# Attention's scores with their 288 rows stacked as 128, 128 and 32, and two spans leaving PSUM in one instruction

## The chip, the core and the metric

The kernel runs on one core of a Trainium2 chip. The metric is device time in microseconds (us) of one execution, from a median of several runs. A core has five engines with their own instruction queues: TensorE (PE: matmuls, with weight loads shown as PEld), VectorE (DVE), ScalarE (ACT), GpSimd (POOL) and SyncE (SP, which here issues DMAs). Matmuls write to PSUM, which has 8 banks of 512 float32 a partition; VectorE and ScalarE read results from there into SBUF.

## The reference

One block of a bidirectional encoder: 1024 tokens of width 1024, with 16 learned tokens ahead of them (1040 keys), a retention branch and a latent attention branch that are merged by gates, then a feed-forward part. The part at hand is the attention of 8 heads. A head's query and key have 64 elements that come from a projection (`nope`) and 32 that are rotated by position (`rope`); the rotated key is shared by all heads.

```python
scale = MLA_QK ** -0.5
...
s = jnp.einsum('bqhd,bkhd->bhqk', qn, k_nope) + jnp.einsum('bqhr,bkr->bhqk', qr, k_rope)
p = jax.nn.softmax(s.astype(jnp.float32) * scale, axis=-1).astype(v.dtype)
return jnp.einsum('bhqk,bkhd->bqhd', p, v)
```

Everything is float32. The kernel multiplies numbers in a rounded float32 type (F32R in the code), and keeps accuracy by splitting an operand into a high part (the rounded number) and a low part (what is left). A product is then three matmuls: high by high, high by low, low by high.

## The kernel before

The program runs in stages: norm and combined projection, retention, latent projections, attention (from about 660 to 936 us), then the output projections and the feed-forward part. Only attention and what feeds it are touched.

*Operands.* For each head there are four SBUF tiles, `q[0]`, `q[1]` (96 x 1024, high and low) and `k[0]`, `k[1]` (96 x 1040). Rows 0 to 63 are the projected part, rows 64 to 95 the rotated part. `heads_begin` loads the rotated rows from DRAM (`qr_d` for queries, written by `rotary` as [half][high or low], and `kr_d` for keys, written by `shared_key`: eight loads a head), `heads_k` and `heads_q` compute the projected rows, in three column chunks each, from latents with a `gemm`; ScalarE rounds the high part, VectorE or GpSimd subtracts to get the low part. Heads come in pairs, and the pair after is prepared while the odd head of a pair is in work.

*Scores.* `softmax` handles one head and one block of 128 queries. The 1040 keys are three spans of 384, 384 and 272 (`ACH`), each in a PSUM bank of its own from the pool `ps_s` with three buffers. Each span is three matmuls of 96 rows (`mm3`, lines 140 to 142):

```python
mm3(ps[:, :n], q[0][:, t], q[1][:, t], k[0][:, c], k[1][:, c], True, True)
dve.tensor_scalar(pr[:, c], ps[:, :n], sq_c[:, qb : qb + 1], None, ALU.mult, ALU.max, accum_out=mx[:, j : j + 1])
```

The second line (line 1142) takes the span out of PSUM, multiplies by the query's norm factor `sq_c`, and leaves the span's maximum in `mx`. Line 1143 takes the maximum of the three with the sign turned (`nm`); line 1144 takes the exponential on ScalarE, in place, with the sum beside it.

*Turning and mixing.* `turn` transposes the eight 128 x 128 parts of a block on TensorE (line 1152, tiles `t`, pool `ps_t` with three buffers), ScalarE rounds them to `pth` (line 1154), VectorE subtracts to get `ptl` (line 1155). `turn_meta` does the same for the 16 extra keys, `inverse` gets the reciprocal of the sums to the right layout through DRAM (`l_d`, `lb`). `mix_values` multiplies the turned blocks by the values: 17 matmuls (lines 1181 and 1182) into a bank `o` of the pool `ps_o` (two buffers).

*Order.* The unit of the loop is one head and 256 queries (two blocks): 32 units. In the loop the scores of the next unit stand ahead of the turning of this one, and the mixing of the last unit comes after the first block's turning. The instructions are recorded by this code and then put in an order by a scheduler of the framework when the program is built; each engine runs its own queue strictly in that order, with semaphores for what one engine needs of another. So what stands next to what on TensorE is read from the built program's order, not from the code.

PSUM's eight banks in attention are three for `s`, three for `t`, two for `o`.

Of the kernel before, what the change touches and what calls it, by code (L numbers as in the profile page):

```python
# [18 lines left out]
NS, NT, NO = 3, 3, 2  # L19
D = 1024  # L20
S = 1024
NM = 16
L = S + NM
H = 8
KT = D // P
NB = S // P
# [4 lines left out]
BANK = {"11": "a", "t2": "b", "t3": "c", "n1": "d", "21": "a", "t4": "c", "22": "d"}  # L31
QCH = ((0, 384), (384, 384), (768, 256))
ACH = ((0, 384), (384, 384), (768, 272))


LINE = 16
# [14 lines left out]
def build(nc, tc, A, out):  # L51
# [26 lines left out]
    load = nc.sync.dma_start  # L78
    store = nc.sync.dma_start

    def f(t):
        return t.bitcast(F32)
# [175 lines left out]
    with ExitStack() as c1:  # L258
# [740 lines left out]
        wt = sb(rot, "rotary", 1, side="right")  # L999
        rr_ = sb(rot, "rotary_r", 11, side="right")  # L1000

        qr_d = [[mk(dram, (P, S), f"qr{i}{j}") for j in range(2)] for i in range(2)]
        wx, xx, tables = [], {}, []

        def wx_load(i):
# [8 lines left out]
        def rotary(lo, n, i):  # L1014
            c = slice(lo, lo + n)
            if i == 0:
                tables[:] = slot(rr_), slot(rr_)
                load(tables[0], A["cM"][:, c])
                load(tables[1], A["sM"][:, c])
            ta, tb_ = slot(rr_), slot(rr_)  # L1020
            dve.tensor_mul(ta, xx[lo, i], tables[0])
            dve.tensor_mul(tb_, xx[lo, 1 - i], tables[1])
            (dve.tensor_add if i else dve.tensor_sub)(ta, ta, tb_)
            hi = tb_.bitcast(F32R)
            act.copy(hi, ta)
            dve.tensor_sub(ta, ta, tb_)
            store(qr_d[i][0][:, c], tb_)
            store(qr_d[i][1][:, c], ta)

        ret_out(0)  # L1030
        seven_out(seven(w7, A["w_ro"][1], Z), cr, ret_post(1))
# [40 lines left out]

    with ExitStack() as c1:
        qk = sb(c1, "qk", 3)
        vp = sb(c1, "v", 1)
        vt = mk(vp, (P, NB + 1, H, P), "vt", F32R)
        pool.memset(f(vt)[:, NB], 0.0)
# [4 lines left out]
        ps_s = sb(c1, "ps_s", NS, space=PSUM)  # L1082
        ps_o = sb(c1, "ps_o", NO, space=PSUM)
        ps_t = sb(c1, "ps_t", NT, space=PSUM)

# [4 lines left out]
        def heads_begin(p):  # L1090
            wq = weights(wa, A["w_uq"][p], 384, "q")
            wk = weights(wa, A["w_uk"][p], 256, "k")
            for h in range(2):
                hh = 2 * p + h
                q = [mk(qk, (96, S), f"q{j}", F32R) for j in range(2)]
                k = [mk(qk, (96, 1152), f"k{j}", F32R)[:, :L] for j in range(2)]
                for j in range(2):
                    load(f(k[j])[64:80], kr_d[j][0:16])
                    load(f(k[j])[80:96], kr_d[j][32:48])
                    for i in range(2):  # L1100
                        load(f(q[j])[64 + 16 * i : 80 + 16 * i], qr_d[i][j][hh * 16 : hh * 16 + 16])
                qk_t[hh] = (q, k)
            return wq, wk

        def heads_k(p, wk, lo, n):
            c = slice(lo, lo + n)
            ps = mk(*((ps_o, (P, 512), "o") if p else (ps_t, (P, 512), "t")))
            gemm(ps[:, :n], wk, ckv, 2, lo, n)
            for h in range(2):
                k = qk_t[2 * p + h][1]  # L1110
                hs = slice(64 * h, 64 * h + 64)
                kf = mk(w2, (64, 384), "kf")
                dve.tensor_mul(kf[:, :n], ps[hs, :n], skv_b[hs, c])
                act.copy(k[0][0:64, c], kf[:, :n])
                pool.tensor_sub(k[1][0:64, c], kf[:, :n], f(k[0])[0:64, c])

        def heads_q(p, wq, lo, n):
            c = slice(lo, lo + n)
            ps = mk(*((ps_o, (P, 512), "o") if p else (ps_t, (P, 512), "t")))
            gemm(ps[:, :n], wq, cq, 3, lo, n)  # L1120
            for h in range(2):
                q = qk_t[2 * p + h][0]
                hs = slice(64 * h, 64 * h + 64)
                act.copy(q[0][0:64, c], ps[hs, :n])
                if p == 0 or h == 0:
                    dve.tensor_sub(q[1][0:64, c], ps[hs, :n], f(q[0])[0:64, c])
# [3 lines left out]
                pool.tensor_sub(q[1][0:64, c], qf[:, :n], f(q[0])[0:64, c])  # L1130

        def softmax(hh, qb, s, sums):
            q, k = qk_t[hh]
            t = slice(qb * P, (qb + 1) * P)
            mx = mk(w4, (P, 3), "mx")
            nm = mk(w4, (P, 1), "nm")
            pr = mk(w4, (P, L), "pr")
            for j, (lo, n) in enumerate(ACH):
                ps = mk(ps_s, (P, 512), "s")
                c = slice(lo, lo + n)  # L1140
                mm3(ps[:, :n], q[0][:, t], q[1][:, t], k[0][:, c], k[1][:, c], True, True)
                dve.tensor_scalar(pr[:, c], ps[:, :n], sq_c[:, qb : qb + 1], None, ALU.mult, ALU.max, accum_out=mx[:, j : j + 1])  # L1142
            dve.tensor_reduce(nm, mx, axis=AX.X, op=ALU.max, negate=True)  # L1143
            act.activation(pr, pr, AF.Exp, bias=nm, accum_out=sums[:, s : s + 1])  # L1144
            return pr

        def turn(pr, s, pt):
# [17 lines left out]
        def inverse(hh, qc, sums):  # L1165
            sm = mk(w4, (P, 2), "sm")
            dve.reciprocal(sm, sums)
            tp = mk(ps_t, (P, 4, P), "t")
            pe.transpose(tp[:2, 0, :], sm, ident)
            rr = mk(w4, (2, P), "rr")  # L1170
            act.copy(rr, tp[:2, 0, :])
            store(l_d[hh, 2 * qc : 2 * qc + 2], rr)
            lb = mk(w4, (64, 256), "lb")
            load(lb, l_d[hh, 2 * qc : 2 * qc + 2].rearrange("b i -> (b i)").unsqueeze(0).broadcast_to([64, 256]))
            return lb

        def mix_values(hh, qc, pt, lb):
            po = mk(ps_o, (P, 512), "o")
            for b in range(NB):
                for j in range(2):  # L1180
                    pe.matmul(po[:, :256], vt[:, b, hh, :], pt[j][:, b, :], start=(b == 0 and j == 0), stop=False)  # L1181
            pe.matmul(po[:, :256], vt[:, NB, hh, :], pt[2], start=False, stop=True)
            ta, tb_ = mk(w2, (64, 256), "oa"), mk(w2, (64, 256), "ob")
            act.copy(ta, po[64:128, :256])
            act.copy(tb_, po[0:64, :256])  # L1185
            pool.tensor_add(ta, ta, tb_)  # L1186
            hs = slice((hh % 2) * 64, (hh % 2) * 64 + 64)
            c = slice(qc * 256, qc * 256 + 256)
            if hh < H - 2:
                pool.tensor_mul(ta, ta, lb)  # L1190
                store(o_d[hh // 2, hs, c], ta)
            else:
                pool.tensor_mul(o3[qc // 2][hs, (qc % 2) * 256 : (qc % 2) * 256 + 256], ta, lb)
# [7 lines left out]
        sums_t, lb_t = {}, {}  # L1201

        def soft(unit, s):
            hh, qc = unit
            if s == 0:
                sums_t[unit] = mk(w4, (P, 2), "sums")
            return softmax(hh, 2 * qc + s, s, sums_t[unit])

        cur = [soft(units[0], s) for s in range(2)]

# [16 lines left out]

        wnext, late, o_s = None, None, []

        def mix(what):  # L1230
            if what:
                hh, qc, pt = what
                mix_values(hh, qc, pt, lb_t[hh, qc])

        for i, (hh, qc) in enumerate(units):
            nxt = units[i + 1] if i + 1 < len(units) else None
# [37 lines left out]
        mix(late)  # L1274


    with ExitStack() as c1:
# [348 lines left out]
```

## Time and profile before

| | us |
|---|---|
| time, median of 3 runs | 1725.82 |
| lowest and highest run | 1722.62, 1725.92 |
| the profiled execution's own time | 1727.16 |
| its span, first to last instruction | 1725.4 |
| stretch 0 to 660 (norm, projections, retention): TensorE busy | 637.5 |
| stretch 690 to 936 (attention): length | 246.0 |
| stretch 936 to the end (output, feed-forward): TensorE busy | 778.1 |

The granted clock of TensorE is at 0.99 to 1.00 throughout. In the rows of the profile a group is `line engine op out<-in`, with the names of the program's tiles; for a matmul `96*128 96x384` means 96 rows by 128 columns of the stationary operand, and 384 columns streamed from 96 rows. A matmul's shown duration includes the way through the array, so that rows that follow each other overlap: what a matmul costs in a stream is the distance to the next one's start. An entry `A <- B` of the waits means that A stood still until B was done.

### The profile page before, as it was taken

The page shows a single profiled execution, that of the slowest core. Times are in us where ns is not written, and L with a number is a line of the kernel's source. Part 1 is how long each engine was busy: PE and PEld are TensorE (multiplying, and loading weights), DVE is VectorE, ACT ScalarE, POOL GpSimd, SP SyncE. Part 2 cuts the span into 40 slices and gives each one's busy share as a digit, 9 for nine tenths or more (in the row PEclk, how much of TensorE's full clock was granted, in tenths as well). Part 3 has the DMA queues.
Part 4 walks back from the last instruction along what each step waited for, and adds up shares of the span by engine and source line. Part 5 has one row for each costly group of instructions (what it writes and reads, how often), then busy time and mean ns, then how long its engine had stood idle before and what let it go on. Part 6 is the DMA issues. An engine that isn't in the chain of part 4 may idle for free.

```text
span 1725.4 us, 26240 instructions
## 1 busy us (share of the span) xinstructions
PE 1686.0 (98%) x8657; PEld 1422.0 (82%) x8657; DVE 1355.5 (79%) x2484; ACT 838.5 (49%) x1581; POOL 740.4 (43%) x562
## 2 busy tenths in 40 slices
PE   9999999999998999999999999999999999999998
PEld 7888777888886777999998888888888888788787
DVE  8856698889899766988897769866788777866865
ACT  7535576433435424788886346333333333522335
POOL 0340377665644421323322401566666665423421
PEclk9999999999999999999999999999999999999999
DMA  8876734565647775111123744333444444876612
GB/s 287 286 272 196 246 129 147 172 219 199 221 140 274 233 243 174 32 49 29 29 84 116 241 151 147 101 101 98 135 146 141 140 147 162 305 269 210 227 59 98
DMA packets 169913, 287.15 MB, mean 166 GB/s; under 512 B 20841, under 2 KB 46882, under 8 KB 169778
## 3 DMA queue, kind: packets, MB, share of 16 engines
q1 hardware_dynamic: 168338, 284.15, 49.4%
q8 instruction: 68, 1.11, 0.3%
q10 hardware_dynamic: 1440, 1.33, 0.2%
q14 instruction: 67, 0.55, 0.1%
HBM read 193.28 MB, written 92.06 MB: 165 GB/s over the span
## 4 chain that ended last, share of the span: by engine, by line
PE 55%; DVE 4%; DMA 3%; ACT 1%; issue 1%; POOL 0%; SPq 0%; DVEq 0%; ACTq 0%
PE mm L223 32%; PE mm L140 3%; PE mm L141 3%; PE mm L142 3%; PE o L1181 3%; PE t L1152 3%; PE s L140 2%; PE s L141 1%; PE s L142 1%; DMA slot<-fl_d 1%; DVE slot L156 1%; DMA slot<-f_d 1%; DVE pr L1142 1%; PE o L140 1%; PE o L141 1%
## 5 line engine op out<-in xcount | busy, mean ns | idle before, releaser
L223 PE MATMUL mm<-slot,slot 128*128 128x512 f32 x2604 | 595.0, 390 | 3.6 <-DVE slot L216 1.8
L223 PEld LDWEIGHTS mm<-slot,slot 128*128 128x128 f32 x2604 | 487.2, 188 | 110.3 <-DVE slot L216 4.4
L216 ACT CAST slot<-slot 128x512 fp32r<-128x512 f32 (+1 forms) x385 | 226.2, 596 | 444.6 <-PE mm L223 345.6
L216 DVE TENSOR_TENSOR slot<-slot,slot 128x512 fp32r<-128x512 f32 (+1 forms) x385 | 351.9, 918 | 69.4 <-ACT slot L216 68.6
L196 POOL TENSOR_TENSOR slot<-slot,slot 128x512 f32<-128x512 f32 (+1 forms) x54 | 78.8, 1459 | 334.9 <-DMA slot<-in_w_g 79.2
L223 PE MATMUL mm<-ht,slot 128*128 128x512 f32 x552 | 184.8, 397 | 4.8 <-ACT slot L216 3.2
L223 PE MATMUL mm<-h,slot 128*128 128x512 f32 x440 | 152.9, 406 | 9.9 <-DVE slot L216 6.8
L214 POOL TENSOR_TENSOR slot<-slot,slot 128x512 f32<-128x512 f32 (+1 forms) x54 | 72.0, 1334 | 144.5 <-DVE slot L216 99.3
L156 DVE TENSOR_TENSOR slot<-slot,slot 128x512 fp32r<-128x512 f32 x123 | 98.9, 822 | 38.1 <-ACT slot L156 35.4
L223 PEld LDWEIGHTS mm<-ht,slot 128*128 128x128 f32 x552 | 103.1, 188 | 28.2 <-ACT slot L216 4.1
L156 ACT CAST slot<-slot 128x512 fp32r<-128x512 f32 x123 | 74.7, 620 | 77.6 <-POOL slot L1326 23.1
L223 PEld LDWEIGHTS mm<-h,slot 128*128 128x128 f32 x440 | 83.8, 192 | 30.9 <-DVE slot L216 9.6
L223 PE MATMUL mm<-lt,slot 128*128 128x512 f32 x276 | 108.5, 393 | 0.0
L141 PE MATMUL mm<-slot,slot 128*128 128x512 f32 (+1 forms) x288 | 105.3, 366 | 0.0
L142 PE MATMUL mm<-slot,slot 128*128 128x512 f32 (+1 forms) x288 | 105.3, 365 | 0.0
L140 PE MATMUL mm<-slot,slot 128*128 128x512 f32 (+1 forms) x288 | 105.2, 367 | 0.0
L1142 DVE TENSOR_SCALAR_CACHE_REDUCE pr<-s,sq_c 128x384 f32<-128x384 f32 (+1 forms) x192 | 101.9, 573 | 3.3 <-PE s L142 1.5
L197 POOL TENSOR_TENSOR slot<-slot,slot 128x512 f32<-128x512 f32 (+1 forms) x54 | 78.2, 1448 | 46.0 <-DVE slot L216 44.1
L1155 DVE TENSOR_TENSOR ptl<-t,pth 128x512 fp32r<-128x512 f32 x128 | 84.6, 685 | 11.3 <-ACT pth L1154 10.3
L223 PE MATMUL mm<-l,slot 128*128 128x512 f32 x220 | 88.1, 401 | 0.0
L1186 POOL TENSOR_TENSOR oa<-oa,ob 64x256 f32<-64x256 f32 x32 | 23.7, 742 | 144.9 <-ACT ob L1185 144.9
L1144 ACT ACTIVATE pr<-pr,nm 128x1040 f32<-128x1040 f32 x64 | 74.5, 1165 | 16.9 <-DVE nm L1143 16.8
(418 smaller groups left out, 3627.2 us busy)
## 6 DMA issues: line engine op xcount, KB each, us to landing
slot<-in_w_in SPq DMA_DIRECT2D x89, 256.0 KB
f_d<-slot SPq DMA_DIRECT2D x71, 256.0 KB
slot<-f_d SPq DMA_DIRECT2D x71, 256.0 KB
slot<-in_xT SPq DMA_DIRECT2D x48, 256.0 KB
slot<-in_w_g SPq DMA_DIRECT2D x44, 256.0 KB
slot<-in_w_u SPq DMA_DIRECT2D x44, 256.0 KB
fl_d<-slot SPq DMA_DIRECT2D x42, 256.0 KB
slot<-fl_d SPq DMA_DIRECT2D x42, 256.0 KB
```

Source lines behind the costliest of these rows:

```text
L140: pe.matmul(ps, sh, mh, start=start, stop=False)
L141: pe.matmul(ps, sh, ml, start=False, stop=False)
L142: pe.matmul(ps, sl, mh, start=False, stop=stop)
L156: split.done = act.copy(hi, t), dve.tensor_sub(lo, t, f(hi))
L196: adds.tensor_add(s1, a21, a22)
L197: adds.tensor_sub(s2, s1, a11)
L214: adds.tensor_sub(s2, s2, a12)
L216: split.done = act.copy(hi, side[b]), dve.tensor_sub(low, side[b], f(hi))
L223: split.mm = pe.matmul(ps, sw[:, ks], sx, start=begins and q == qs[0] and i == 0, stop=q == nq - 1 and i == 2, skip_group_check=True)
L1142: dve.tensor_scalar(pr[:, c], ps[:, :n], sq_c[:, qb : qb + 1], None, ALU.mult, ALU.max, accum_out=mx[:, j : j + 1])
L1144: act.activation(pr, pr, AF.Exp, bias=nm, accum_out=sums[:, s : s + 1])
L1155: dve.tensor_sub(pt[1][d], tp, f(pt[0])[d])
```

## The change

*Rows.* A score is a sum over 288 products of rows: 64 projected and 32 rotated, three times each. Before, they are three matmuls of 96 rows. Now they are two matmuls of 128 rows and one of 32. `q[0]` holds the projected high part over the projected low part, against `k[0]`, which holds the projected high part twice. `q[1]` holds projected high, rotated high and rotated low, against projected low, rotated low and rotated high in `k[1]`. What is left is rotated high by rotated high, 32 rows. The doubled rows are copied from SBUF to SBUF by SyncE's DMAs (one in `heads_k` and one in `heads_q` for each head and column chunk).

*The 32 rows.* The rotated high keys are loaded once into `kr` (96 x 384): the 32 rows of span 0 at partitions 0 to 31, of span 1 at 32 to 63, of span 2 at 64 to 95. The rotated high queries of a unit are loaded three times, to the same three places, into `rq` (three loads a unit, pool `ro` with three buffers). So the 32-row matmuls of the three spans lie on different rows of the array. `qr_d` gets another shape, so that a head's 32 rows are one load.

*Spans and PSUM.* The spans are 352, 352 and 336. The first two lie in one two-bank tile `s` (pool `ps_s`, one buffer), the third in a bank `u` (pool `ps_u`, one buffer). One VectorE instruction takes 704 columns out of `s`, one takes 336 out of `u`. The norm factor now carries a minus sign, so the instruction keeps a minimum, and the exponential turns the sign back.

*Mixing.* The 17 matmuls of `mix_values` are recorded in two portions, 8 after the first block's turning and 9 after the second's. `mx`, `rr` and `lb` get two buffers in place of four.

```diff
-    latent_norm(sq_c, 3, 96.0**-0.5, range(NB))
+    latent_norm(sq_c, 3, -(96.0**-0.5), range(NB))
...
+        kr = mk(vp, (96, 384), "kr", F32R)
+        for j, n in enumerate(SPANS):
+            for i in range(2):
+                load(f(kr)[32 * j + 16 * i : 32 * j + 16 * i + 16, :n],
+                     kr_d[0][32 * i : 32 * i + 16, SN * j : SN * j + n])
+        ps_s = sb(c1, "ps_s", 1, space=PSUM)
+        ps_u = sb(c1, "ps_u", 1, space=PSUM)
...
+                load(f(k[0])[64:128, c], f(k[0])[0:64, c])
...
+                load(f(q[1])[0:64, c], f(q[0])[0:64, c])
...
+        def rotary_queries(hh, qc):
+            t = mk(ro, (96, 256), "rq", F32R)
+            for j in range(3):
+                load(f(t)[32 * j : 32 * j + 32],
+                     qr_d[0][hh, :, :, qc * 256 : qc * 256 + 256].rearrange("i r t -> (i r) t"))
+            return t
...
-            for j, (lo, n) in enumerate(ACH):
-                ps = mk(ps_s, (P, 512), "s")
-                c = slice(lo, lo + n)
-                mm3(ps[:, :n], q[0][:, t], q[1][:, t], k[0][:, c], k[1][:, c], True, True)
-                dve.tensor_scalar(pr[:, c], ps[:, :n], sq_c[:, qb : qb + 1], None, ALU.mult, ALU.max, accum_out=mx[:, j : j + 1])
+            pa, pb = mk(ps_s, (P, 2, 512), "s"), mk(ps_u, (P, 512), "u")
+            spans = [(ps, slice(SN * j, SN * j + n)) for j, (ps, n) in
+                     enumerate(zip((pa[:, 0, :SN], pa[:, 1, :SN], pb[:, : SPANS[2]]), SPANS))]
+            for ps, c in spans:
+                for i in range(2):
+                    pe.matmul(ps, q[i][:, t], k[i][:, c], start=i == 0, stop=False)
+            for j, (ps, c) in enumerate(spans):
+                r = slice(32 * j, 32 * j + 32)
+                softmax.mm = pe.matmul(ps, rq[r, s * P : s * P + P], kr[r, : SPANS[j]], start=False, stop=True)
+            col = sq_c[:, qb : qb + 1]
+            dve.tensor_scalar(pr[:, : 2 * SN].rearrange("p (j n) -> p j n", n=SN), pa[:, :, :SN], col, None,
+                              ALU.mult, ALU.min, accum_out=mx[:, 0:1])
+            dve.tensor_scalar(pr[:, 2 * SN :], pb[:, : SPANS[2]], col, None, ALU.mult, ALU.min, accum_out=mx[:, 1:2])
...
-                if s == 0:
-                    mix(late)
+                mix(late, s, nxt)
```

The work ahead of attention and behind it keeps its order. Inside attention, TensorE's queue at one block of scores in the middle of the first head (tiles with their numbers; `s` are scores, `o` the mixing, `t` the transposes), before:

```order
L140 MATMUL s_7279<-k_1408_6774,q_1406_6772 128x384
L141 MATMUL s_7279<-k_1409_6775,q_1406_6772 128x384
L142 MATMUL s_7279<-k_1408_6774,q_1407_6773 128x384
L140 MATMUL s_7284<-k_1408_6774,q_1406_6772 128x384
L141 MATMUL s_7284<-k_1409_6775,q_1406_6772 128x384
L142 MATMUL s_7284<-k_1408_6774,q_1407_6773 128x384
L140 MATMUL s_7289<-k_1408_6774,q_1406_6772 128x272
L141 MATMUL s_7289<-k_1409_6775,q_1406_6772 128x272
L142 MATMUL s_7289<-k_1408_6774,q_1407_6773 128x272
L1182 MATMUL o_7251<-ptm_1399_6742,vt_6739 128x256
L1152 MATMUL t_7296<-ident_60,pr_7168 128x128 x4
L1152 MATMUL t_7303<-ident_60,pr_7168 128x128 x4
```

And the same block now (`kr` and `rq` are the operands of 32 rows):

```order
L1165 MATMUL s_7284<-k_1407_6785,q_1405_6783 128x352
L1165 MATMUL s_7284<-k_1408_6786,q_1406_6784 128x352
L1165 MATMUL s_7284<-k_1407_6785,q_1405_6783 128x352
L1165 MATMUL s_7284<-k_1408_6786,q_1406_6784 128x352
L1168 MATMUL s_7284<-kr_6746,rq_7236 128x352 x2
L1165 MATMUL u_7285<-k_1407_6785,q_1405_6783 128x336
L1165 MATMUL u_7285<-k_1408_6786,q_1406_6784 128x336
L1168 MATMUL u_7285<-kr_6746,rq_7236 128x336
L1182 MATMUL t_7299<-ident_60,pr_7173 128x128 x4
L1219 MATMUL o_7272<-ptm_1397_6743,vt_6740 128x256
L1182 MATMUL t_7306<-ident_60,pr_7173 128x128 x4
L1199 MATMUL t_7331<-ident_60,sm_7329 2x128
```

The code records the three 32-row matmuls behind all six others, but the scheduler has put the third span's two 128-row matmuls between the second and the third of them: the 32-row matmuls stand in 127 separate places for 64 blocks (two places a block, one in the first block). VectorE's queue at the same block, before:

```order
L1142 TENSOR_SCALAR pr_7278,mx_7276<-s_7279,sq_c_77 128x384
L1142 TENSOR_SCALAR pr_7278,mx_7276<-s_7284,sq_c_77 128x384
L1142 TENSOR_SCALAR pr_7278,mx_7276<-s_7289,sq_c_77 128x272
L1143 TENSOR_REDUCE nm_7277<-mx_7276 128x1
L1155 TENSOR_TENSOR ptl_7215<-t_7296,pth_7214 128x4x128
L1155 TENSOR_TENSOR ptl_7215<-t_7303,pth_7214 128x4x128
```

And now:

```order
L1170 TENSOR_SCALAR pr_7283,mx_7281<-s_7284,sq_c_77 128x704
L1172 TENSOR_SCALAR pr_7283,mx_7281<-u_7285,sq_c_77 128x336
L1173 TENSOR_REDUCE nm_7282<-mx_7281 128x1
L1185 TENSOR_TENSOR ptl_7234<-t_7299,pth_7233 128x4x128
L1185 TENSOR_TENSOR ptl_7234<-t_7306,pth_7233 128x4x128
L1197 RECIPROCAL sm_7439<-sums_7235 128x2
```

The three evictions have become two, at the same place in the queue; what follows them is unchanged.

More of the change, by code (lines that the diff above doesn't have):

```diff
@@ L18 @@
 P = 128
-NS, NT, NO = 3, 3, 2
+NT, NO = 3, 2
 D = 1024
@@ L33 @@
 ACH = ((0, 384), (384, 384), (768, 272))
+SN, SPANS = 352, (352, 352, 336)
 LINE = 16
@@ L1000, in build @@
         rr_ = sb(rot, "rotary_r", 11, side="right")
-        qr_d = [[mk(dram, (P, S), f"qr{i}{j}") for j in range(2)] for i in range(2)]
+        qr_d = [mk(dram, (H, 2, 16, S), f"qr{j}") for j in range(2)]
         wx, xx, tables = [], {}, []
@@ L1026, in rotary @@
             dve.tensor_sub(ta, ta, tb_)
-            store(qr_d[i][0][:, c], tb_)
-            store(qr_d[i][1][:, c], ta)
+            store(qr_d[0][:, i, :, c], tb_)
+            store(qr_d[1][:, i, :, c], ta)
         ret_out(0)
@@ L1074, in build @@
         qk = sb(c1, "qk", 3)
+        ro = sb(c1, "rotary_q", 3)
         vp = sb(c1, "v", 1)
@@ L1081, in build @@
             pool.memset(f(t), 0.0)
-        ps_s = sb(c1, "ps_s", NS, space=PSUM)
+        kr = mk(vp, (96, 384), "kr", F32R)
[5 more added lines that the diff above has]
+        ps_u = sb(c1, "ps_u", 1, space=PSUM)
         ps_o = sb(c1, "ps_o", NO, space=PSUM)
@@ L1094, in heads_begin @@
                 hh = 2 * p + h
-                q = [mk(qk, (96, S), f"q{j}", F32R) for j in range(2)]
-                k = [mk(qk, (96, 1152), f"k{j}", F32R)[:, :L] for j in range(2)]
+                q = [mk(qk, (P, S), f"q{j}", F32R) for j in range(2)]
+                k = [mk(qk, (P, 1152), f"k{j}", F32R)[:, :L] for j in range(2)]
                 for j in range(2):
-                    load(f(k[j])[64:80], kr_d[j][0:16])
-                    load(f(k[j])[80:96], kr_d[j][32:48])
                     for i in range(2):
-                        load(f(q[j])[64 + 16 * i : 80 + 16 * i], qr_d[i][j][hh * 16 : hh * 16 + 16])
+                        r = slice(64 + 32 * j + 16 * i, 80 + 32 * j + 16 * i)
+                        load(f(k[1])[r], kr_d[1 - j][32 * i : 32 * i + 16])
+                    load(f(q[1])[64 + 32 * j : 96 + 32 * j], qr_d[j][hh].rearrange("i r t -> (i r) t"))
                 qk_t[hh] = (q, k)
@@ L1133, in softmax @@
+        def softmax(hh, qb, s, sums, rq):
             q, k = qk_t[hh]
             t = slice(qb * P, (qb + 1) * P)
-            mx = mk(w4, (P, 3), "mx")
+            mx = mk(w2, (P, 2), "mx")
             nm = mk(w4, (P, 1), "nm")
             pr = mk(w4, (P, L), "pr")
-            for j, (lo, n) in enumerate(ACH):
-                ps = mk(ps_s, (P, 512), "s")
-                c = slice(lo, lo + n)
-                mm3(ps[:, :n], q[0][:, t], q[1][:, t], k[0][:, c], k[1][:, c], True, True)
-                dve.tensor_scalar(pr[:, c], ps[:, :n], sq_c[:, qb : qb + 1], None, ALU.mult, ALU.max, accum_out=mx[:, j : j + 1])
@@ L1145, in softmax @@
+            dve.tensor_reduce(nm, mx, axis=AX.X, op=ALU.min)
+            act.activation(pr, pr, AF.Exp, bias=nm, scale=-1.0, accum_out=sums[:, s : s + 1])
             return pr
@@ L1169, in inverse, with mix_begin, mix_some, mix_values @@
             pe.transpose(tp[:2, 0, :], sm, ident)
-            rr = mk(w4, (2, P), "rr")
+            rr = mk(w2, (2, P), "rr")
             act.copy(rr, tp[:2, 0, :])
             store(l_d[hh, 2 * qc : 2 * qc + 2], rr)
-            lb = mk(w4, (64, 256), "lb")
+            lb = mk(w2, (64, 256), "lb")
             load(lb, l_d[hh, 2 * qc : 2 * qc + 2].rearrange("b i -> (b i)").unsqueeze(0).broadcast_to([64, 256]))
             return lb
-        def mix_values(hh, qc, pt, lb):
+        def mix_begin(hh, qc, pt):
             po = mk(ps_o, (P, 512), "o")
-            for b in range(NB):
+            mix_some(po, hh, pt, range(4))
+            return po
+        def mix_some(po, hh, pt, bs):
+            for b in bs:
                 for j in range(2):
                     pe.matmul(po[:, :256], vt[:, b, hh, :], pt[j][:, b, :], start=(b == 0 and j == 0), stop=False)
+        def mix_values(po, hh, qc, pt, lb):
+            mix_some(po, hh, pt, range(4, NB))
             pe.matmul(po[:, :256], vt[:, NB, hh, :], pt[2], start=False, stop=True)
@@ L1200, in build @@
         units = [(hh, qc) for hh in range(H) for qc in range(4)]
-        sums_t, lb_t = {}, {}
+        sums_t, lb_t, rq_t = {}, {}, {}
         def soft(unit, s):
@@ L1206, in soft @@
                 sums_t[unit] = mk(w4, (P, 2), "sums")
-            return softmax(hh, 2 * qc + s, s, sums_t[unit])
+                rq_t[unit] = rotary_queries(hh, qc)
+            return softmax(hh, 2 * qc + s, s, sums_t[unit], rq_t[unit])
         cur = [soft(units[0], s) for s in range(2)]
@@ L1228, in build, with mix @@
         wnext, late, o_s = None, None, []
-        def mix(what):
-            if what:
+        open_ = []
+        def mix(what, s, nxt):
+            if not what:
+                return
+            if s == 0:
+                open_.append(mix_begin(*what))
+            else:
                 hh, qc, pt = what
-                mix_values(hh, qc, pt, lb_t[hh, qc])
+                mix_values(open_.pop(), hh, qc, pt, lb_t[hh, qc])
         for i, (hh, qc) in enumerate(units):
@@ L1273, in build @@
             cur = new
-        mix(late)
+        for s in range(2):
+            mix(late, s, None)
     with ExitStack() as c1:
```

7 lines of the change are left out of this document (2 added, 5 removed).

## The prediction

> **What bounds the kernel now.** I read the page's head first, then the table by stretches of time, then who waits for whom inside the attention stage, then the instructions of TensorE in order of time. The profiled execution took 1727.16 us, with a span of 1725.4, so 1.8 us lie around the span; the sum below starts from 1727.16, which stands 1.3 us above the median of 1725.82. Page and stretches (microseconds, then busy time and count of each engine):
>
> ```profile
> PE 1686.0 (98%) x8657; PEld 1422.0 (82%) x8657; DVE 1355.5 (79%) x2484; ACT 838.5 (49%) x1581; POOL 740.4 (43%) x562
> ...
> 660.00:690.00 30.00, 27.75 (x149) 23.91 (x148) 20.91 (x50) 16.49 (x30) 7.12 (x9) 1.00 0.40 117
> 690.00:936.00 246.00, 242.67 (x1824) 234.78 (x1824) 220.22 (x661) 199.47 (x437) 70.25 (x89) 1.00 0.15 44
> ```
>
> The change touches only attention, which is the stretch from 690 to 936 with its start from 660. There TensorE is busy 242.7 of 246.0 us at full clock, and VectorE 220.2. What TensorE waits for in that stretch is short (total, times, longest):
>
> ```profile
> PEld s L140 <- DVE pr L1142: 2.4, 8, 0.5
> PEld o L1181 <- ACT pth L1154: 2.1, 4, 0.7
> PEld t L1160 <- ACT rr L1171: 1.6, 4, 0.5
> ```
>
> So in attention time is what TensorE's queue adds up to. One block of scores, TensorE's rows in order (start, duration):
>
> ```profile
> 746.47 0.34 PE L140 MATMUL s<-k,q 96*128 96x384 f32 x1
> 746.65 0.34 PE L141 MATMUL s<-k,q 96*128 96x384 f32 x1
> ...
> 747.52 0.28 PE L140 MATMUL s<-k,q 96*128 96x272 f32 x1
> 747.64 0.29 PE L141 MATMUL s<-k,q 96*128 96x272 f32 x1
> 747.77 0.29 PE L142 MATMUL s<-k,q 96*128 96x272 f32 x1
> 747.89 0.29 PE L1182 MATMUL o<-ptm,vt 128*128 128x256 f32 x1
> 748.02 1.04 PE L1152 MATMUL t<-ident,pr 128*128 128x128 f32 x8
> 748.89 0.27 PE L1169 MATMUL t<-ident,sm 128*2 128x128 f32 x1
> ```
>
> Durations overlap, so cost is start to start. The nine matmuls of a block take 747.89 - 746.47 = 1.42 us: six of 384 columns at (747.52 - 746.47)/6 = 0.175, three of 272 at 0.123. There are 64 blocks.
>
> **The change, part by part.** *Streaming.* A column costs (0.175 - 0.123)/112 = 0.46 ns, so 352 columns cost 0.160 us and 336 cost 0.152. The six full-height matmuls take 4 x 0.160 + 2 x 0.152 = 0.944. Behind them come three of 32 rows. In the new order two stand next to each other and the third alone, behind the full-height ones of its own span. Matmuls on different rows of the array are in the trace: the retention stage has pairs of 64 rows (L744), one on rows 0 to 63 and one on 64 to 127 (two records for each matmul). Rows at 413 us, and the durations (min/median/max) of all of L744:
>
> ```profile
> 413.96 0.39 PE L223 MATMUL mm<-lt,slot 128*128 128x512 f32 x1
> 414.19 0.40 PE L223 MATMUL mm<-ht,slot 128*128 128x512 f32 x1
> 414.52 1.33 PE L744 MATMUL mm<-rq,rk 64*128 64x128 f32 x16
> 415.78 0.50 PE L223 MATMUL mm<-ht,slot 128*128 128x512 f32 x1
> 416.12 0.40 PE L223 MATMUL mm<-lt,slot 128*128 128x512 f32 x1
> ...
> L744 PE MATMUL mm<-rq,rk x128: 272/272/373, 295.4 to 471.0; 64*128 64x128 f32 x128
> ```
>
> The 16 start (1.33 - 0.37)/15 = 0.064 us apart; full-height ones of the same 128 columns, the eight transposes at 748.02, (1.04 - 0.27)/7 = 0.11 apart. So neighbours on different rows run side by side. Two 32-row matmuls then cost little over one, 0.17, and the third 0.152. Streaming alone goes from 1.42 to 0.944 + 0.32 = 1.264, a gain of 0.156 a block, **-10.0 us** in all.
>
> *Changing the height.* The same rows show what it costs to go to partial rows and back. At one height the start after 414.19 would be 0.23 later, at 414.42; the first 64-row matmul starts at 414.52, and takes 0.373 instead of 0.272. By ends: 414.59 for the last full one, 414.52 + 0.37 = 414.89 for the first partial one, of which its 128 columns stream 0.06; the array streams nothing for 0.24 us. On the way back the sixteen end at 415.85 and the next full one at 416.28, 0.43 later where 0.23 is usual: 0.20. No wait explains it, since the weight load ahead of the sixteen is put down to its own issue:
>
> ```profile
> 414.51 1.14 PEld L744 LDWEIGHTS mm<-rq,rk 64*128 64x128 f32 x16 [0.36 <-issue]
> ```
>
> Its start at 414.51 also shows that it was not pulled ahead of the running matmul, as the others are. A visit to another height thus costs 0.24 + 0.20 = 0.44 us beyond its streaming. In the new order a block makes two visits, one for the pair and one for the third; once in the program all three stand together, so 127 visits: **+55.9 us**. Nothing hides it, since TensorE is what everything waits for. Those rows have 64 rows of unrounded operands; 32 rows of rounded ones (F32R in the code) do not occur, so the bounds are 0 and 0.44 a visit. There is a row on the side of 0: a narrow rounded operand (48 columns of the stationary side, `um`) between full ones.
>
> ```profile
> 97.15 0.61 PE L603 MATMUL mm<-slot,h 128*128 128x512 f32 x2
> 97.60 0.40 PE L606 MATMUL mm<-slot,um 128*48 128x512 f32 x1
> 97.83 0.39 PE L223 MATMUL mm<-ht,slot 128*128 128x512 f32 x1
> 98.06 0.40 PE L223 MATMUL mm<-lt,slot 128*128 128x512 f32 x1
> ```
>
> Starts lie 0.23 apart throughout, so a narrower width is free there. I take 0.44, because L744 is the nearest row in kind (a part of the rows, not of the columns, and operands that start at another row).
>
> [...]
>
> *Leaving PSUM.* VectorE's rows of the stretch 690 to 936 (busy, mean ns of one):
>
> ```profile
> L1142 DVE TENSOR_SCALAR_CACHE_REDUCE pr<-s,sq_c 128x384 f32<-128x384 f32 x122 | 70.7, 612 | 3.2 <-PE s L142 1.5 <-PE t L1160 1.0
> L1142 DVE TENSOR_SCALAR_CACHE_REDUCE pr<-s,sq_c 128x272 f32<-128x272 f32 x61 | 30.2, 495 | 0.0
> L1142 DVE DVE_READ_ACCUMULATOR pr<-s,sq_c 128x1 f32 x183 | 15.1, 82 | 0.0
> ```
>
> Three evictions take 2 x 0.612 + 0.495 = 1.72 us. At (0.612 - 0.495)/112 = 1.04 ns a column, 704 columns take 0.945 and 336 take 0.56: 1.51. VectorE gains 0.21 a block, 13 us in all, and a short accumulator read. It is not late for TensorE (2.4 us of waits), so I count nothing.
>
> *The wait it adds.* The pair of banks `s` has one buffer; the next block's first matmul waits for the whole 704-column eviction, and everything behind it on TensorE waits too. At the narrowest place stand, between the pair's last matmul and the next block, three matmuls of the third span (0.46), eight transposes (0.88), one `o` (0.12) and one short one (0.03): 1.49 us, and 0.64 of switching. Needed are 0.945, about 0.17 until the matmul's end, and up to 0.60 if VectorE has just begun a `ptl` (899.00 to the next start at 899.60):
>
> ```profile
> 899.00 0.68 DVE L1155 TENSOR_TENSOR ptl<-t,pth 128x512 fp32r<-128x512 f32 x1
> 899.60 0.60 DVE L1142 TENSOR_SCALAR_CACHE_REDUCE pr<-s,sq_c 128x384 f32<-128x384 f32 x1
> ```
>
> That is 1.72 of 2.13: hidden. Without the switches up to 0.23 would show, once in each of 32 units, 7 us at most.
>
> *Loads.* SyncE gets 96 loads of `rq`, 48 copies inside SBUF and six of `kr`, and loses 16. Beside that stand its issue times now, and its waits in the stretch:
>
> ```profile
> L1101 SPq DMA_DIRECT2D q<-qr x32: 303/418/1664, 667.1 to 838.2; - x32
> ...
> SPq L1172 <- ACT rr L1171: 79.3, 18, 6.7
> SPq L1191 <- POOL oa L1190: 46.9, 17, 7.0
> SPq L1174 <- DMA l_d<-rr: 16.8, 22, 1.8
> ```
>
> 134 x 0.42 = 56 us fit in 126 us of waiting, and three `rq` buffers let a load start two units, some 14 us, ahead: nothing. Were that cover gone and each unit waited as long as the worst small store (1.8 us), it would be 58 us. The half-and-half mixing keeps its 17 matmuls, the sign moves no work: nothing.
>
> *The start.* All of V's matmuls now stand ahead of the first 32-row ones, so the first evictions no longer lie beside them. The three next blocks wait for a one-buffer pair; between 0 and 6 us, I take +2. TensorE's short waits, 3.3 us in the stage, partly vanish under the switching: -2.
>
> Sum: -10.0 + 55.9 + 2 - 2 = +45.9, so 1727.2 + 45.9 = **1773 us**.
>
> **The rivals.** *No switch cost, side by side (faster).* If rounded matmuls switch height as freely as L606 switches width, only streaming counts: 1727.2 - 10.0 + 2 = 1719, up to 1726 with the PSUM wait. It decides from the point where a visit costs less than 10.0/127 = 0.08 us. For it: L606. Against it: L744, both ways. *No switch cost, one after the other.* If they neither drain nor overlap, a block costs 0.944 + 2 x 0.160 + 0.152 = 1.416 against 1.42: nothing gained, 1729 with the start. Here the change does not do what its words say. *Cheap switch.* If only the late start counts (0.10 each way, the weights loading meanwhile), 127 x 0.20 = 25.4, less 10: 1743. [...]
>
> **How the numbers follow.** Full switch 0.54 (own range 1758 to 1783: 0.35 to 0.50 us a visit), cheap switch 0.10, free and side by side 0.21, free and serial 0.15. A measurement of this kernel tells about 0.2%, 3.5 us, from no change. Leaving out the free case would leave out over 2 in 10, so the range runs from 1716 to 1783. Faster 0.20 (nearly all of the free case), same 0.12 (most of the serial one), slower 0.68.
>
> **What would show it.** Behind a pair of 32-row matmuls on TensorE: an end 0.4 us after the one ahead, and a weight load not pulled ahead, mean full switch; starts 0.16 apart mean a free one. Two 32-row starts 0.01 apart mean side by side, 0.16 serial. Eviction rows near 0.95 and 0.56 us bear out VectorE's term, TensorE waiting for `pr` over 3 us in the stage would refute the cover, and a wait for `rq` the loads. The prediction is wrong if attention does not grow to some 292 us.

## The result, and the profile after

The changed kernel takes **1767.66 us** (median of 4 runs, 1765.99 to 1771.18) beside 1725.78 of the kernel before (1722.62 to 1725.92): a ratio of 1.025 [1.023, 1.027], 41.9 us slower. The forecast was 1773. The profiled execution took 1771.18 us, with a span of 1769.4.

The stretches of the changed kernel (length, then busy time and count of PE, PEld, DVE, ACT, POOL, then TensorE's clock):

```profile
660.00:690.00 30.00, 30.00 (x148) 25.32 (x147) 18.56 (x31) 12.85 (x24) 7.21 (x9) 1.00 0.56 169
690.00:936.00 246.00, 244.52 (x1580) 198.34 (x1578) 186.91 (x471) 175.77 (x372) 61.55 (x77) 0.99 0.23 63
936.00:978.00 42.00, 41.25 (x282) 33.23 (x282) 35.40 (x85) 32.68 (x71) 8.76 (x12) 1.00 0.21 62
```

In the 246 us that attention took before, TensorE now gets through 1580 matmuls in place of 1824 and is as busy as before; attention goes on to 978. VectorE's busy time in that stretch falls from 220.2 to 186.9.

To measure the stage alike in every run I take its first and last mark on other engines: the first start of VectorE's `kf<-t` (first keys) and the last start of ScalarE's `oa` (last mixed block). In these rows stand durations (min/median/max, ns), then first and last start. Before:

```profile
L1113 DVE TENSOR_TENSOR kf<-t,skv_b x6: 432/546/560, 667.4 to 673.3; 64x384 f32<-64x384 f32 x4, 64x272 f32<-64x272 f32 x2
L1184 ACT COPY oa<-o x32: 352/369/371, 699.2 to 936.0; 64x256 f32<-64x256 f32 x32
```

And after:

```profile
L1125 DVE TENSOR_TENSOR kf<-t,skv_b x6: 424/547/559, 672.6 to 678.7; 64x384 f32<-64x384 f32 x4, 64x272 f32<-64x272 f32 x2
L1221 ACT COPY oa<-o x32: 369/369/372, 710.0 to 978.3; 64x256 f32<-64x256 f32 x32
```

So attention starts 672.6 - 667.4 = **5.2 us later** and lasts 305.7 us in place of 268.6, **37.1 more**. What follows it grows by 1.7 (1769.4 - 978.3 against 1725.4 - 936.0). Together 44.0, the whole difference of the two spans.

Not all of the 37.1 us is work. Early in the stage TensorE's granted clock is low for a while (the number behind the five engines):

```profile
690.00:702.00 12.00, 10.87 (x42) 6.99 (x39) 6.68 (x19) 6.21 (x9) 0.00 (x0) 0.72 0.42 110
```

In the kernel before it is 1.00 in these 12 us. At 0.72 up to 12 x 0.28 = 3.4 us are lost. Over 690 to 936 the clock reads 0.99 in the change, one_visit and three_visits, in all of which a block's 32-row matmuls lie on different rows; it reads 1.00 in the kernel before, full_height, no_third, same_rows, both_undone and the two probes. What sets it off was not tested.

One block of scores, TensorE's rows in order of time (start, duration):

```profile
750.44 0.88 PE L1165 MATMUL s<-k,q 128*128 128x352 f32 x4
751.25 0.43 PE L1168 MATMUL s<-kr,rq 32*128 32x352 f32 x2
751.61 0.57 PE L1165 MATMUL u<-k,q 128*128 128x336 f32 x2
752.11 0.41 PE L1168 MATMUL u<-kr,rq 32*128 32x336 f32 x1
752.46 0.39 PE L1215 MATMUL o<-pth,vt 128*128 128x256 f32 x1
```

The two 32-row matmuls together take 0.43 us where one of them takes 0.41: they run side by side, and start 0.01 us apart or less. But the last full-height one ends at 750.44 + 0.88 = 751.32 and the pair at 751.68, 0.36 later, of which its 352 columns stream 0.16: 0.20 in which the array streams nothing. On the way to the third: the full-height one ends at 752.18, the 32-row one at 752.52, 0.34 for 336 columns worth 0.15: 0.19. On the way back the `o` ends at 752.85, 0.33 later for 256 columns that take 0.12 in a stream: 0.21. The weight loads of the same stretch, with what each stood still for:

```profile
750.41 0.62 PEld L1165 LDWEIGHTS s<-k,q 128*128 128x128 f32 x4
751.25 0.18 PEld L1168 LDWEIGHTS s<-kr,rq 32*128 32x128 f32 x2 [0.21 <-issue]
751.61 0.30 PEld L1165 LDWEIGHTS u<-k,q 128*128 128x128 f32 x2 [0.17 <-DVE ptl L1185]
752.11 0.18 PEld L1168 LDWEIGHTS u<-kr,rq 32*128 32x128 f32 x1 [0.21 <-issue]
```

The load of the first full-height weights stands ahead of its matmul, at 750.41. Each 32-row load starts with its own matmul and waits for no other engine. (The 0.17 at 751.61 is named after VectorE's `ptl`, but on the full-height way back the same 0.2 appears as plain issue elsewhere, below.) The waits of the stage from 690 to 978 (total, times, longest):

```profile
PEld s L1168 <- issue: 14.7, 66, 0.4
...
PEld u L1168 <- issue: 12.6, 59, 0.4
...
PEld u L1165 <- issue: 5.3, 31, 0.2
...
PEld o L1215 <- ACT pth L1184: 1.3, 5, 0.3
PEld s L1168 <- DMA rq<-qr: 1.3, 2, 1.0
PEld s L1165 <- DVE pr L1170: 1.2, 2, 0.9
...
PEld t L1190 <- ACT rr L1201: 1.0, 3, 0.5
```

The 32-row weights stood still 125 times, by (14.7 + 12.6)/125 = 0.22 us, for nothing but the issue: this is the switch. A load takes 0.18 us, and here it starts only with its matmul, so the 0.2 may be a load that nothing hides; these rows do not show what the 0.22 is made of. The two waits that the change might have brought, for `rq` and for the one-buffer pair of banks (`s` waiting for `pr`), come to 1.3 and 1.2 us, two times each. VectorE's evictions:

```profile
L1170 DVE TENSOR_SCALAR_CACHE_REDUCE pr<-s,sq_c 128x704 f32<-128x704 f32 x64 | 60.7, 948 | 18.6 <-PE t L1190 9.4 <-PE s L1168 8.7
L1172 DVE TENSOR_SCALAR_CACHE_REDUCE pr<-u,sq_c 128x336 f32<-128x336 f32 x64 | 36.0, 563 | 2.5 <-PE u L1168 2.5
```

They cost 0.948 and 0.563 us, and 18.6 us of idle time now stand ahead of the first: what VectorE gains, it waits away.

### The profile page after: what moved, and what is told of

The parts are those of the page before. It is cut to its first block, busy times and chain, and to the rows that moved or that the text cites. A ratio compares the mean times of both kernels' runs of the same rounds, so it can differ in the third digit from the quotient of the medians.

```text
span 1769.4 us, 26331 instructions
## 1 busy us (share of the span) xinstructions
PE 1725.6 (98%) x8657; PEld 1414.1 (80%) x8657; DVE 1351.7 (76%) x2356; ACT 842.1 (48%) x1581; POOL 739.9 (42%) x562
## 5 line engine op out<-in xcount | busy, mean ns | idle before, releaser
L225 PE MATMUL mm<-ht,slot 128*128 128x512 f32 x552 | 186.9, 401 | 8.1 <-ACT slot L218 4.5
L1184 ACT CAST pth<-t 128x512 fp32r<-128x512 f32 x128 | 71.7, 585 | 42.2 <-PE t L1182 41.8
```

The source lines that it names most:

```text
L225: split.mm = pe.matmul(ps, sw[:, ks], sx, start=begins and q == qs[0] and i == 0, stop=q == nq - 1 and i == 2, skip_group_check=True)
L1184: act.copy(pt[0][d], tp)
```

## The experiments

Each ratio is to the kernel before in the same set of runs (medians of 1725.78 to 1727.62 there), with its 95% interval. The stage runs from `kf` to `oa`, as above, in the profiled execution.

| run | time (us) | ratio to before, interval | stage starts | stage lasts |
|---|---|---|---|---|
| kernel before | 1725.78 | | 667.4 | 268.6 |
| the change | 1767.66 | 1.025 [1.023, 1.027] | 672.6 | 305.7 |
| one_visit | 1744.37 | 1.0107 [1.0076, 1.0138] | 671.3 | 280.0 |
| three_visits | 1806.45 | 1.0471 [1.0437, 1.0505] | 672.4 | 339.8 |
| full_height | 1733.55 | 1.0038 [1.0023, 1.0052] | 671.1 | 270.2 |
| no_third | 1715.86 | 0.9937 [0.9909, 0.9965] | 670.8 | 251.6 |
| same_rows | 1773.65 | 1.0266 [1.0242, 1.0289] | 671.0 | 311.5 |
| probe32 | 1757.35 | 1.0177 [1.0151, 1.0202] | 665.8 | 296.5 |
| probe96 | 1737.56 | 1.0056 [1.0037, 1.0076] | 668.7 | 276.8 |
| old_qr | 1762.76 | 1.0198 [1.0169, 1.0226] | 669.0 | 306.6 |
| new_qr | 1732.28 | 1.0033 [1.0022, 1.0044] | 669.7 | 268.7 |
| after_again | 1769.62 | 1.0244 [1.0220, 1.0267] | 672.5 | 305.6 |
| both_undone | 1727.95 | 1.0001 [0.9989, 1.0014] | 667.5 | 271.7 |

### The price of a change of height, alone: probe32 and probe96

To the kernel before, one matmul of zeros is added behind the third span's three, 64 in the program. Once it has 32 rows, once 96, the height of its neighbours; the columns streamed are the same.

```diff
-mm3(ps[:, :n], q[0][:, t], q[1][:, t], k[0][:, c], k[1][:, c], True, True)
+mm3(ps[:, :n], q[0][:, t], q[1][:, t], k[0][:, c], k[1][:, c], True, j != 2)
+if j == 2:
+    pe.matmul(ps[:, :n], q[0][:32, t], zr, start=False, stop=True)   # 96 in probe96
```

Expected of 32 rows:

> The kernel before, and behind the last span's three matmuls one more of 32 rows by 272 columns of zeros into the same bank, 64 in all: the disputed cost by itself. Theory: 64 x (0.37 + 0.124) = 32 us more than before, 1757 us. Rival 1 (a change of height is free): 64 x 0.124 = 8 more, 1734. Rival 2 (0.22 for each 32-row matmul beyond streaming): 22 more, 1748.

Expected of 96 rows:

> The same probe with 96 rows of zeros, so no change of height: the streaming alone. All theories: 64 x 0.124 = 8 us more than before, 1734 us.

Measured: 1757.35 and 1737.56, a difference of 19.8 us, or **0.31 us a visit**; by the stages it is 19.7. The 96 rows cost their stream of 64 x 0.123 = 8 us and a little (8.2 by the stage, 10.6 by the time over the 1726.97 beside it). In the 32-row run all 64 have the same duration; its rows (min/median/max in ns, then first and last start):

```profile
L1145 PE MATMUL s<-zr,q x64: 385/385/388, 676.8 to 951.9; 32*128 32x272 f32 x64
```

At full height:

```profile
L1145 PE MATMUL s<-zr,q x64: 283/289/293, 679.6 to 935.4; 96*128 96x272 f32 x64
```

One place of the 32-row run on TensorE:

```profile
752.84 0.29 PE L142 MATMUL s<-k,q 96*128 96x272 f32 x1
753.05 0.39 PE L1145 MATMUL s<-zr,q 32*128 32x272 f32 x1
753.37 0.39 PE L1186 MATMUL o<-ptm,vt 128*128 128x256 f32 x1
```

The one matmul takes 0.10 us longer than its neighbour of the same columns, starts 0.21 after it in place of 0.12 to 0.13, and the next starts 0.32 later. The operands are rounded and nothing else was added, so this decides against the two free rivals: a visit costs four times the 0.08 us below which the change would have paid.

### How often: one_visit, three_visits

The three 32-row matmuls are held together behind all six full-height ones (64 visits), or each is put behind its own span's two (192).

```diff
+with tc.issue_after(full.ins):          # full: the last full-height matmul, of the block or of the span
     ... the 32-row matmul(s)
```

> The changed kernel with one edit: all three 32-row matmuls of a block are held behind its last full-height matmul, so that they stand together: 64 places instead of 127. Theory (each place where TensorE changes height costs about 0.37 us beyond streaming, as the rows after the change show): 63 x 0.37 = 23 us less, and the third one beside the pair instead of alone, 63 x 0.15 = 9.5 less: 1735 us, up to 1739 if the later eviction shows. Rival 1 (the loss comes from the one-buffer pair of PSUM banks or from the new loads): no gain, 1767 or a little more, since eviction starts later. Rival 2 (each 32-row matmul costs its own, 42/192 = 0.22 us, however they stand): 1768.

> The changed kernel with one edit: each span's 32-row matmul stands behind that span's own two full-height ones: 192 places instead of 127. Theory: 65 x 0.37 = 24 us more, and the pair no longer side by side, 64 x 0.15 = 9.5 more: 1801 us. Rival 1 (PSUM pair or loads): 1768. Rival 2 (cost for each 32-row matmul): 1768, 1777 with the pair's streaming.

Measured: 1744.37 and 1806.45. Time follows the number of visits, 64, 127, 192, with stages of 280.0, 305.7 and 339.8 us. From 127 to 192 visits it is 34.1 us; less the 0.16 x 64 of pairs that no longer run side by side, 0.37 a visit. three_visits came 5 us over its forecast of 1801. **one_visit is a miss by 5 to 9 us.** By 63 visits fewer at 0.37, and 64 thirds now beside a pair at 0.15, its stage should be 32.9 us shorter than that of the change, and is 25.7 shorter. What its TensorE's weight loads wait for in the stage:

```profile
PEld s L1165 <- DVE pr L1171: 3.5, 7, 0.8
PEld o L1216 <- ACT pth L1185: 3.3, 6, 1.3
PEld t L1191 <- ACT rr L1202: 2.4, 5, 0.8
```

These three come to 9.2 us; in the change the same three were 1.2, 1.3 and 1.0, 3.5 in all. That is 5.7 of the 7.2 us that are missing: with half of the switches out, waits that they had covered appear to come up; the rest is open.

### No change of height: full_height

The third product takes all 128 rows of `q[1]` against a copy of the keys that is zero outside the rotated high rows: the same sum, without `rq` and without a partial matmul.

```diff
-    softmax.mm = pe.matmul(ps, rq[r, s * P : s * P + P], kr[r, : SPANS[j]], start=False, stop=True)
+    softmax.mm = pe.matmul(ps, q[1][:, t], kr[:, c], start=False, stop=True)     # kr 128 x 1040, mostly zeros
```

> The changed kernel, but the rotated high by rotated high product is done in 128 rows: the second stationary operand again, against a tile that is zero outside the 32 rows. No partial rows in attention, no rq loads; PSUM tiles, evictions and mixing as in the changed kernel. Theory: 127 x 0.37 = 47 us less, streaming 64 x 0.152 = 10 more: 1731 us, beside the 1726 of before. Rival 1 (the one-buffer pair): 1768 or more. Rival 1b (the rq loads): also about 1731, told apart by whether 32-row starts in the changed kernel wait for loads.

Measured: 1733.55, a stage of 270.2 us against 268.6 before. With 127 visits gone, 34 of the 42 us are gone, at the price of streaming one more matmul a block. (Up to 3.4 of the 34 are the clock, which is 1.00 here from 690 to 936.) But of the 6.2 us that it still is over the kernel before beside it (1727.39), the stage holds 1.6 and the late start, 671.1, 3.7.

### No third product: no_third

The three 32-row matmuls are left out, and nothing takes their place.

> The changed kernel without the rotated high by rotated high product: the two full-height matmuls of each span are all that is left of the scores (the rq and kr loads stay). Theory: 127 x 0.37 = 47 us and 64 x 0.32 = 20 us of streaming less: 1700 us, up to 1706 where VectorE or the one-buffer pair becomes the bound. Rival 1 (PSUM pair or loads): 1747, the streaming alone. Rival 2: 1700 as well.

Measured: 1715.86, **a miss by 10 us or more**. A block then costs 0.944 us of TensorE in place of 1.42, 30 us in all, but the stage is only 17.0 us shorter than before. What the weight loads wait for:

```profile
PEld o L1212 <- ACT pth L1181: 5.3, 10, 1.1
PEld s L1165 <- DVE pr L1167: 5.0, 10, 0.9
PEld t L1187 <- ACT rr L1198: 3.1, 7, 1.4
```

The same three are 2.1, 2.4 and 1.6 in the kernel before (the prediction shows them); they grow by 7.3 of the 13.5 us that are missing. VectorE and ScalarE are close behind TensorE (busy for 218.9 and 208.2 of the 246 us from 690, TensorE for 235.8): of 30 us taken from it, little over half arrives. By this run, no arrangement of the 32-row matmuls can bring this design more than some 17 us in the stage, and to bring that they would have to be free.

### Side by side or not: same_rows

All three 32-row matmuls use rows 96 to 127, so that no two lie on different rows; visits stay at 127, and `rq` takes one load a unit.

```diff
-    softmax.mm = pe.matmul(ps, rq[r, s * P : s * P + P], kr[r, : SPANS[j]], start=False, stop=True)
+    softmax.mm = pe.matmul(ps, rq[96:128, s * P : s * P + P], k[1][96:128, c], start=False, stop=True)
```

> The changed kernel with the 32-row matmuls of all three spans on the same rows, 96 to 127 (the keys' rotated high rows are there already in the second key tile; rq is one load a unit instead of three). Still 127 places. Theory (the pair runs side by side in the changed kernel): 64 x 0.15 = 9.5 us more, 1777 us. Rival (the pair does not overlap anyway): 1768. If the loads cost anything: less than either.

Measured: 1773.65, by the ratios 0.0016 to 0.0022 above the change in its two measurements (3 to 4 us, with intervals that overlap); by the stages 5.8 us longer. The rows of one pair on TensorE:

```profile
752.60 0.81 PE L1158 MATMUL s<-k,q 128*128 128x352 f32 x4
753.34 0.58 PE L1160 MATMUL s<-k,rq 32*128 32x352 f32 x2
753.85 0.57 PE L1158 MATMUL u<-k,q 128*128 128x336 f32 x2
```

The pair takes 0.58 us in place of 0.43, and the next matmul starts 0.51 us after it in place of 0.36: side by side is real and gains 0.15 us a block, as expected. The stage grew by less than 64 times that because this run lacks the change's low clock (1.00 from 690 to 936): 5.8 + 3.4 = 9.2 us, or 0.14 a block. This run also has two loads of `rq` a unit fewer, and what that gives back wasn't measured alone.

### The start: old_qr, new_qr, after_again

The runs up to here agree in one thing that no theory so far had: with the probes attention starts at 666 to 669, with every version of the change at 671 to 673. TensorE's queue ahead of attention holds the same work in the same order in all of them. What differs there is one of SyncE's operations: `rotary` stores its queries into `qr_d` of another shape. SyncE's rows for it before (durations, first and last start):

```profile
L1027 SPq DMA_DIRECT2D qr<-slot x4: 319/350/384, 625.1 to 637.7; - x4
L1028 SPq DMA_DIRECT2D qr<-slot x4: 319/323/369, 626.3 to 639.8; - x4
```

And after:

```profile
L1029 SPq DMA_DIRECT2D qr<-slot x4: 577/592/694, 626.9 to 640.7; - x4
L1030 SPq DMA_DIRECT2D qr<-slot x4: 577/622/1194, 628.1 to 643.7; - x4
```

The destination is no longer one block of 128 rows but 8 times 16 rows, and each issue takes 0.59 to 0.62 us in place of 0.32 to 0.35. Eight of them, and what is queued behind them on SyncE comes later; among that is a load of `slot<-g_d` (at 647.16 in place of 641.47), for which VectorE waits 5.6 us at a stretch, where its longest such wait before was 3.6. In order of time on TensorE, the changed kernel:

```profile
650.24 0.39 PE L225 MATMUL mm<-lt,slot 128*128 128x512 f32 x1
653.62 1.22 PE L225 MATMUL mm<-ht,slot 128*128 128x512 f32 x2 [2.99 <-DVE slot L218]
654.64 0.63 PE L225 MATMUL mm<-lt,slot 128*128 128x512 f32 x1
655.07 1.05 PE L225 MATMUL mm<-ht,slot 128*128 128x512 f32 x2
...
658.90 0.91 PE L225 MATMUL mm<-hn,slot 128*128 128x512 f32 x2
659.65 0.39 PE L225 MATMUL mm<-ln,slot 128*128 128x512 f32 x1
659.88 0.39 PE L225 MATMUL mm<-hn,slot 128*128 128x512 f32 x1
```

TensorE stands still for 2.99 us, and then its matmuls start 0.43 us apart (654.64 to 655.07) in place of 0.23 (659.65 to 659.88), until 658.90. Two kernels tell the shape from a drift between runs: the change with `qr_d`'s old shape, and the kernel before with the new one.

```diff
-qr_d = [mk(dram, (H, 2, 16, S), f"qr{j}") for j in range(2)]
+qr_d = [[mk(dram, (P, S), f"qr{i}{j}") for j in range(2)] for i in range(2)]
...
-store(qr_d[0][:, i, :, c], tb_)
+store(qr_d[i][0][:, c], tb_)
```

Expected with the old shape in the change:

> The changed kernel with one part undone: qr_d keeps its shape of before, so each store of rotated queries is one plain 128 x 512 block again (0.33 us of SyncE's queue in the kernel before, 0.58 to 0.69 now), and rq takes six loads a unit in place of three. Theory: the stores of the new shape push SyncE's later loads back (g_d stands 5.7 us later at 647.16 against 641.47), VectorE waits for that slot and TensorE for VectorE (3 us in place of 1 near 649), and attention starts some 5 us late. Then attention starts near 662 to 664 again, its stage stays at 308 us, and the time is 1763, some 4 us under the changed kernel in the same runs. Rival: the late start is drift between runs, and the time is that of the changed kernel, 1768. Second rival: the doubled rq loads show as a wait of TensorE for rq, and the time is above 1768.

Expected with the new shape in the kernel before:

> The kernel before with that part alone: qr_d in the new shape, everything in attention as before (the loads of rotated queries read the same rows from the new places). Theory: attention starts 4 to 5 us later at an unchanged length of 274 us, and the time is 1731 against 1727. Rival (drift between runs): 1727, no difference.

Expected of the change, beside them:

> The changed kernel itself beside the two, so that the three are compared on one chip: 1768 by every theory; it gives the distance to the first of these runs, 4 to 5 us by the theory of the stores and none by drift.

Measured: old_qr 1762.76, 6.9 us under after_again's 1769.62 though it issues twice the loads of `rq` (their intervals, 1.0169 to 1.0226 and 1.0220 to 1.0267, just touch); new_qr 1732.28, 5.0 us over the 1727.28 of the kernel before in the same runs, with an interval of 1.0022 to 1.0044. In new_qr the stage keeps its length (268.7 us) and starts at 669.7, 2.3 us later where 4 to 5 were expected; in old_qr it starts 3.5 us before after_again's, where some 5 were expected. The wait of TensorE in new_qr between 630 and 662, where the kernel before has 2.0 us (total, times, longest):

```profile
PE mm L223 <- DVE slot L216: 5.3, 2, 4.2
```

The longest of these is a stop that every profile with the new shape has, 2.9 to 4.2 us long; in the change, new_qr, one_visit and full_height its end is put down to that slot. With the old shape no wait for that slot between 630 and 662 is longer than 1.4 us in the kernel before, old_qr and the probes, and in both_undone TensorE is busy for 13.94 of the 14 us from 648 to 662. In old_qr the wait is 0.5, and TensorE's clock stays whole:

```profile
648.00:660.00 12.00, 11.52 (x51) 9.23 (x50) 6.87 (x11) 2.41 (x4) 0.00 (x0) 1.00 0.90 346
```

So by these medians a new shape of eight stores costs 5 to 7 us, ahead of the stage that the change is about. With the shape the scheduler also exchanges two neighbours on VectorE and moves one load of weights by a place on SyncE, alike in the change and in new_qr; what part of the cost is theirs was not taken apart.

### What is left: both_undone

full_height with `qr_d`'s old shape: rows of 128 and 128, the new spans, two evictions, the one-buffer banks, the copies and the mixing in portions stay.

> The changed kernel without any 32-row matmul (the third product takes q[1]'s 128 rows against keys that are zero outside 32 of them, as in the run full_height) and with qr_d's stores in their shape of before. What is left of the change is 128 + 128 rows, spans of 352, 352 and 336, two evictions a block, a one-buffer pair of banks, the copies inside SBUF and the mixing in two portions. Theory: the visits and the stores are all that the change costs, so the time is that of the kernel before, 1727 to 1729 (full_height's 1733.5 less about 5), and attention is 274 us from a start near 662. Rival: something else in it costs or gains a few us (the one-buffer wait, or VectorE's two evictions), and the time is off 1727 by over 3.5 us.

Measured: 1727.95 against 1727.62, a ratio of 1.0001 [0.9989, 1.0014]. So, to within some 2 us, the 32-row matmuls (with the low clock that goes with them) and the stores are the whole cost, and the rest of the change is worth nothing either way. The stage of its profile is 3.1 us longer than before, but that execution, at 1731.14, was itself 3.2 us over the run's median.

No version that computes the whole score beat the kernel before. One with three 32-row matmuls side by side once a block costs TensorE 0.944 + 0.17 + 0.37 = 1.48 us by the numbers above, against 1.42. One visit for two blocks would cost less by the same numbers, but needs six banks for scores, where these kernels have three; it was not tried.

## Why the prediction was right, and where not

- **Changing the height: right that it costs, size too high.** The term was 0.44 us a visit, 55.9 in all. The probe measured 0.31, the extra visits of three_visits 0.37, and the rows of the one block above 0.19 to 0.20 in and 0.20 to 0.21 out. The stage's 37.1 us, with the streaming of -10.0 kept, give (37.1 + 10.0)/127 = 0.37, 47 us in all; without the up to 3.4 us of low clock, for which the sum had no term, 0.34 and 44 us. The 0.44 was read from unrounded 64-row operands, whose way in cost 0.24; here it is 0.20. Why the probe comes to less than the rows of one place is open. These runs show a loss at every change of height, 0.19 to 0.21 us each way in that block, but not what it is made of: a weight load of 0.18 us stands beside it, and no run tells how much of the loss is the load's.
- **Streaming: right, from a row that does not decide.** The pair runs side by side, within 0.02 us of one, and same_rows bears out the 0.15 us a block. But L744, from which it was read, fits serial matmuls as well: by the prediction's 0.46 ns a column 128 columns stream in 0.059 us, and its sixteen start 0.064 apart on average. The transposes beside it, 0.11 apart, don't show the pace of one height: 256 columns of `o` go at 0.12.
- **Leaving PSUM: right.** 0.948 and 0.563 us against 0.945 and 0.56 predicted from two widths, and counted at nothing; both_undone bears the nothing out.
- **The wait it adds: hidden, as worked out.** TensorE's waits for `pr` fell from 2.4 to 1.2 us, twice in the stage. In one_visit, with half of the switches gone, it is 3.5, inside the 7 us that the prediction allowed without switches.
- **Loads: right in attention, wrong ahead of it; this is the step that failed.** The loads and copies that the change adds cost about 1 us. But the step counted only new DMAs, and passed over stores that were there before and got another shape. They cost 5 to 7 us, where the prediction had nothing. The term for the start (+2) looked for a delay inside attention only. What the profile shows there is the low clock, up to 3.4 us, and about 1 us of waits at the first block (0.44 for `rq`, 0.63 for `pr`).
- **TensorE's vanishing waits (-2): about right.** The three rows that the prediction showed fell from 6.1 us (2.4, 2.1, 1.6) to 3.5.
- **The sum** of +45.9 is over the 41.9 that came, because the switch was set 9 to 12 us too high (55.9 against 44 to 47), while the late start was set 3 us too low (+2 against 5.2) and the low clock and 1.7 us behind attention were not in it. So it is in part luck that the time falls into the full switch's own range (1758 to 1783): errors of both signs cancel. The whole range, 1716 to 1783, holds the time of every rival, so that lying in it tells nothing of the cause; the probes do.
- **The rivals:** the two free ones end with probe32, in which 64 visits alone cost 20 us more than 64 matmuls. The cheap switch (0.20 a visit) lies under everything measured. The last test was that attention grow from 246 to some 292 us; it grew by 37.1 and not by 46, by the size of the switch.

## What to carry to other kernels

Count how often TensorE's queue changes between full and partial height, in the built order and not in the code: here each visit cost 0.3 to 0.4 us, so a few partial matmuls side by side don't pay against full-height ones unless their saving is larger than that. Look at every DMA whose access pattern changes, the stores of an earlier stage too, and at what stands behind it on its queue. Read the granted clock of a stage before its length is put down to work: here up to 3.4 us of clock hid a third of what same_rows was to show. When a bound engine is relieved by 30 us, ask how far behind the next ones are: here it was 17.

## What was not expected of the hardware

**A stop of 2.99 us was followed by 2.5 us lost at a low clock.** After standing still for 2.99 us, the changed kernel's matmuls of 512 columns take 658.90 - 653.62 = 5.3 us for twelve where twelve take 12 x 0.23 = 2.8: another 2.5 us. The clock of that stretch:

```profile
652.00:660.00 8.00, 6.38 (x16) 5.04 (x17) 4.99 (x8) 0.62 (x1) 0.00 (x0) 0.57 0.95 380
```

This is part of how eight stores, each some 0.27 us slower to issue, grew into 5 us. But length alone doesn't decide. In one_visit the stop at the same place is longer, and the clock is 1.00 in every 2 us from 650 to 660:

```profile
651.75 0.73 PE L225 MATMUL mm<-ht,slot 128*128 128x512 f32 x2 [3.69 <-DVE slot L218]
652.32 0.39 PE L225 MATMUL mm<-lt,slot 128*128 128x512 f32 x1
652.55 0.62 PE L225 MATMUL mm<-ht,slot 128*128 128x512 f32 x2
```

Of the eight profiles with this stop, six have a low clock right behind it: the change, and new_qr, after_again, three_visits, full_height and same_rows, where 2 us of it read 0.50. The stop was 2.99 us in the change and 4.2 in new_qr; in the other four TensorE stood idle for 3.53, 3.43, 3.43 and 3.30 us, in that order, of the 14 from 648 to 662. In one_visit (3.69) and no_third (2.94) the clock stayed at 1.00. What sets it off was not tested.
